# Decoder layer on one core: down-weight sums of the first feed-forward part from DRAM to DRAM, X sums kept on chip, output splits in the first down product

## The chip, the cores and the metric

The kernel runs on one core of a Trainium2 chip, in one launch. The metric is the device time of that launch in microseconds (us); lower is better. The time before is the median of three runs. TensorE (PE) multiplies matrices, VectorE (DVE), ScalarE (ACT) and GpSimd (POOL) do the elementwise work, and DMA transfers are issued through queues: SyncE's (SP) for weights and intermediates, GpSimd's for the sums of down weights.

## The reference

One layer in float32, for a sequence of 512 tokens with model width 1024 and feed-forward width 2816 (22 tiles of 128, taken as 11 pairs):

```
def swiglu(x, w_gate, w_up, w_down):
    return (jax.nn.silu(x @ w_gate) * (x @ w_up)) @ w_down

h = rms_norm(x, ffn1_pre)
x = x + 0.5 * rms_norm(swiglu(h, ffn1_w_gate, ffn1_w_up, ffn1_w_down), ffn1_post)
h = rms_norm(x, mix_pre)
x = x + rms_norm(token_mixer(h, ...), mix_post)     # sparse and dilated attention, gated
h = rms_norm(x, ffn2_pre)
x = x + 0.5 * rms_norm(swiglu(h, ffn2_w_gate, ffn2_w_up, ffn2_w_down), ffn2_post)
```

## The kernel before

**Matrix products.** Each float32 operand is split into a high part, cast by ScalarE (line 125), and the rest, subtracted by VectorE (line 126). `mm3` adds three matmuls for a product: high by high, high by low, low by high (lines 148, 149, 150). Both feed-forward parts run through one function, `ffn`, and multiply 2x2 blocks by a scheme of seven products in place of eight, with sums of blocks as operands. A pair of tiles of the gate and up weights takes the products P1, P2, P6, P5, P7, P4, P3, of 24 matmuls with 256 columns each: 168 matmuls a pair. `prep` makes a product's weight operand ready two products ahead: a block of 128x1024, or a sum of blocks (line 488 makes the first of these, for P6), then the split into `whi` and `wlo`.

**Weights.** All weight blocks come through SP's queue, in the order of use, into a ring `raw` of six half tiles. `refill` (line 311) issues the next block when the one before it in that half tile has been used, so a block's issue stands on SP's queue between the stores that other code puts there.

**Outputs of a pair.** `finished` copies the product banks (line 523, ScalarE), adds them and applies silu. After P3, `sums` makes from the two outputs `ev` and `od` three operands for the down products: X (in the one buffer `CB`, or in `PT`), the sum kept in `ev` and Y (lines 388 to 391, VectorE). `od`, X and Y are stored to DRAM (lines 392, 394, 397, SP's queue); where X of a pair is kept on chip it is listed in `kept`, which holds pairs 4 to 10 in the second part and none in the first. `ev` is cast and split at once into two slots named by `E_TAGS`. The first two pairs run without the seven products of the scheme ("plain"), pairs 2 to 10 in the loop.

**Sums of down weights.** The down projection is again seven products, B11, T2, T3, T1, B21, B22, T4, over the 11 pairs each. Four of them take sums of quarters of the down weight, which the kernel makes itself in `td`: td[2] and td[3] of two quarters each, td[0] = td[2] plus another one, td[1] = td[0] plus another one. For the second part, the mixer makes them in `table_sums`: copies and accumulating transfers on GpSimd's queue, from DRAM to DRAM, three pairs in one transfer, five steps for a group. In the first part `weight_sums` makes them as the loop goes: GpSimd's queue loads quarters of one pair into `PT` slots (line 361), accumulates other quarters onto them (line 351, an accumulating transfer too), and at the next step SP's queue stores the results to `td` (line 356). What each step does is listed in `SUMS`. `sums_behind` puts a one-column copy on GpSimd that reads an operand of the pair just finished, and lets the step's transfers be issued only after that copy and after the last store of `od`.

**Down products.** `product` in `ffn_down` goes through the pairs two at a time: split of the weight block, refill, matmuls, and after each pair a call of `side`, which splits the stored operands of later products (`split_next`, staged back from DRAM by `stage`). In B11 it splits an X at every second pair. In the last product T4 the `side` function is `settle`: after pairs 1 and 2 it updates a token tile of the residual x (line 761, whose factor GpSimd computes as a power, line 169), after pair 3 it finishes both tiles (norm, transposes or output). In T4 the weights of the last six pairs are only split as they come, and held: their matmuls follow for one token tile after the other (`tail` is 6).

A scheduler sets the order of each engine's instructions from the program's order and its own costs; the code gives the priority and the dependences. A slot is free again when the last reader of its content is done.

Of the kernel before, what the change touches and what calls it, by code (L numbers as in the profile page):

```python
# [12 lines left out]
F32 = mybir.dt.float32  # L13
# [14 lines left out]
NF = DFF // P  # L28
# [7 lines left out]
SUMS = [((0, 1), (), ())] + [((n + 1,), (n,) if n > 1 else (0, 1), (n - 1,) if n > 2 else (0, 1) * (n == 2)) for n in range(1, 13)]  # L36
# [11 lines left out]
E_TAGS = ["Q"] * 4 + ["KA"] * 4 + ["KB"] * 4 + ["x"] * 8 + ["of"] * 2  # L48
T_TAGS = ["SP"] * 11 + ["dm"]
# [9 lines left out]
class Layer:  # L59
# [257 lines left out]
    def ffn(self, gu, wd, td, post, finish, xsrc, aside=None, opened=None):  # L317
# [5 lines left out]
        later = {}  # L323
# [24 lines left out]
        def weight_sums(n):  # L348

            put = nc.gpsimd.dma_start  # L350
            add = lambda dst, src: put(dst, src, accum_op=OP.add)
            part = lambda q, e, h: wd[e, h, :, q]
            store, self.unstored = self.unstored, []
            keep = lambda i, q, t: self.unstored.append((td[i, :, q], t))
            for dst, t in store:
                nc.sync.dma_start(dst, t)
            new, one, two = [[q for q in v if q < NP] for v in SUMS[n]]
            for q in new:
                later[q] = r = [self.slot("PT") for _ in range(2)]
                for e in range(2):  # L360
                    put(r[e], part(q, e, 1))
            for h, qs in ((1, one), (0, two)):
                for q in qs:
                    add(later[q][0], part(q, 1, h))
                    keep(1 - h, q, later[q][0])
            for q in new:
                r = later[q]
                add(r[1], part(q, 0, 1))
                add(r[0], part(q, 0, 0))
                for e in range(2):  # L370
                    keep(2 + e, q, r[e])

# [11 lines left out]
        def sums(p, ev, od):  # L384

            h = slice(0, 256), slice(256, 512)
            x, y = self.slot("CB" if opened or p < KEEP else "PT"), self.slot("ring")
            nc.vector.tensor_sub(x[:, h[0]], ev[:, h[1]], od[:, h[1]])
            nc.vector.tensor_sub(x[:, h[1]], ev[:, h[0]], ev[:, h[1]])
            nc.vector.tensor_sub(ev[:, h[1]], x[:, h[0]], ev[:, h[0]])  # L390
            nc.vector.tensor_add(y[:, 0:256], od[:, h[0]], ev[:, h[1]])
            self.last_store = nc.sync.dma_start(self.odram[p], od).ins
            if opened or p < KEEP:
                nc.sync.dma_start(self.sxdram[p], x)
            else:
                kept[p] = x
            nc.sync.dma_start(self.ydram[p // 2][:, h[p % 2]], y[:, 0:256])
            hi, lo = [self.slot(e_tags.pop(0), F32R) for _ in range(2)]
            self.split(hi, lo, ev)
            E.append((hi, lo))  # L400

        def extra(p):
            if opened:
                sums_behind(E[p][0][:, 0:1].bitcast(F32), p + 1)

        def sums_behind(src, n):
            mark = self.sbt("mark", [P, 1])
            behind = nc.gpsimd.tensor_copy(mark, src).ins
            with self.tc.issue_after(behind), self.tc.issue_after(self.last_store or behind):
                weight_sums(n)  # L410

        banks = dict(opened["banks"]) if opened else {}
        if opened:
            tops = opened["tops"]
            self.unstored, self.last_store = [], None
# [58 lines left out]
        def last_sums():  # L474
            if opened:
                weight_sums(len(SUMS) - 1)

# [40 lines left out]
        def finished(p, name):  # L518
# [35 lines left out]
        self.ffn_down(E, kept, wd, td, post, finish, xsrc, aside, opened, last_sums)  # L554
# [78 lines left out]
    def ffn_down(self, E, kept, wd, td, post, finish, xsrc, aside, opened, last_sums):  # L633
# [36 lines left out]
        def product(a, wname, banks, start, stop, side=None, tail=0, keep=None, between=None):  # L670
# [8 lines left out]
            for k0 in range(0, NP, 2):  # L679
# [3 lines left out]
                if keep and k0 + m > NP - tail:  # L683
                    for j in range(m):
                        w = [self.slot(keep.pop(0), F32R) for _ in range(2)]
                        self.split(w[0], w[1], src[:, j])
                        held.append((k0 + j, w))
                    self.refill(r)
                    continue
                hi, lo = self.wsplit(src, [m, S])  # L690
                self.refill(r)
                for j in range(m):
# [20 lines left out]

        a = [self.bank("F") for _ in range(2)]
        product(half(E, 0), "B11", a, True, False, lambda k: k % 2 == 0 and split_next("X"))
# [7 lines left out]
        last_sums()  # L723
# [473 lines left out]
    def table_sums(self, wd, td, call):  # L1197

        put = self.nc.gpsimd.dma_start
        for b in range(0, NF // 2, 3):  # L1200
            q = slice(b, min(b + 3, NF // 2))
            step = call - b
            if step in (0, 1):
                for i, e, h in ((2, 0, 1), (3, 1, 1), (0, 1, 1), (1, 1, 0))[2 * step:2 * step + 2]:
                    put(td[i, :, q], wd[e, h, :, q])
            elif step == 2:
                put(td[2, :, q], wd[0, 0, :, q], accum_op=OP.add)
                put(td[3, :, q], wd[0, 1, :, q], accum_op=OP.add)
            elif step == 3:
                put(td[0, :, q], td[2, :, q], accum_op=OP.add)  # L1210
            elif step == 4:
                put(td[1, :, q], td[0, :, q], accum_op=OP.add)
# [415 lines left out]
    def run(self, out):  # L1628
# [10 lines left out]
        def boundary(post, pre, store, tags=None, shift=0):  # L1639
# [3 lines left out]
            def finish(t, gain):  # L1643
# [3 lines left out]
                if pre is not None:  # L1647
# [8 lines left out]
                   lambda m: self.table_sums(a["d2"], td[1], m))  # L1656
# [43 lines left out]
```

## Time and profile before

| what | value |
|---|---|
| runs shown | 1145.02, 1139.07, 1142.3 us; median 1142.3 |
| the profiled execution: its time, its span | 1139.46 us, 1137.7 us |
| granted TensorE clock, mean | 0.997 |
| busy in the span: PE, DVE, ACT, POOL | 97%, 78%, 56%, 15% |
| moved by DMA | 227.54 MB: 185.72 MB on SP's queue, 40.38 MB on GpSimd's |

The span runs from the first to the last instruction. The opening takes until about 37 us, the plain pairs until 51.65, the loop of the first part until about 239, its seven down products until about 362; the mixer follows, and the second part's loop lies within 844 to 1000 us, its down products behind it until the end. A row of a timeline gives the start, the duration, engine and line, the operation and its operands, and in brackets how long the engine had been idle ahead of it and whose end released it. L numbers are the line numbers of the kernel. "PEclk" is the clock that TensorE was granted, as a share of the full one; "x12" counts instructions that began in a stretch.

### The profile page before, as it was taken

What the parts mean: (1) busy time and instruction counts of PE and PEld (TensorE: products, weight loads), DVE (VectorE), ACT (ScalarE), POOL (GpSimd) and SP (SyncE); (2) the same over time, 40 slices, a digit from 0 to 9 for tenths busy, and PEclk for the clock granted to TensorE, in tenths of its full rate; (3) what the DMA queues carried; (4) which work ended last, traced back from release to release, by engine and by line L of the source; (5) the groups of instructions that cost most, each with busy time, mean ns of one, the idle gap of its engine ahead of it and who ended that gap; (6) DMA issues with size and microseconds to landing.
All of it is one profiled execution on the core that took longest, in us unless ns stands there. A gap on an engine that the chain in (4) does not pass through costs nothing.

```text
span 1137.7 us, 18596 instructions
## 1 busy us (share of the span) xinstructions
PE 1103.4 (97%) x6863; PEld 978.9 (86%) x6863; DVE 882.2 (78%) x1554; ACT 639.4 (56%) x1151; POOL 168.2 (15%) x220
## 2 busy tenths in 40 slices
PE   8989999999999999999999999999999999999996
PEld 7889999987878987777888898887989999998884
DVE  5979999987777889687554566876888989879564
ACT  7445555565564778676555634644435555557452
POOL 0423222230011054564000000000000000000000
PEclk9999999999999999999999999999999999999999
DMA  9999999999864669995134425383234434379761
GB/s 348 269 251 273 267 280 264 285 338 315 296 189 133 189 208 283 294 260 118 53 115 131 122 85 157 121 292 135 78 116 135 144 117 148 112 221 327 255 201 75
DMA packets 118411, 227.54 MB, mean 200 GB/s; under 512 B 21904, under 2 KB 51632, under 8 KB 118320
## 3 DMA queue, kind: packets, MB, share of 16 engines
q1 hardware_dynamic: 105472, 185.72, 49.1%
q0 software_dynamic: 12704, 40.38, 15.4%
q8 instruction: 54, 0.88, 0.3%
q14 instruction: 37, 0.30, 0.1%
q10 hardware_dynamic: 144, 0.26, 0.1%
HBM read 191.66 MB, written 57.72 MB: 219 GB/s over the span
## 4 chain that ended last, share of the span: by engine, by line
PE 64%; DVE 16%; DMA 9%; issue 5%; ACT 4%; POOL 2%; SPq 0%; DVEq 0%; POOLq 0%; ACTq 0%
PE pb_F L150 8%; PE pb_F L149 8%; PE pb_F L148 8%; DVE wlo L126 5%; PE pb_S L150 5%; PE pb_S L149 5%; PE pb_S L148 5%; PE pb_T L149 4%; PE pb_T L150 4%; PE pb_T L148 4%; DMA raw<-in_gu_dram 3%; PE pb_V L148 2%; PE pb_V L149 2%; DMA tdram<-in_d_dram 2%; PE pb_V L150 2%
## 5 line engine op out<-in xcount | busy, mean ns | idle before, releaser
L126 DVE TENSOR_TENSOR wlo<-raw,whi 128x1024 fp32r<-128x1024 f32 (+2 forms) x237 | 281.1, 1189 | 117.9 <-ACT whi L125 112.1
L125 ACT CAST whi<-raw 128x1024 fp32r<-128x1024 f32 (+2 forms) x237 | 241.5, 1021 | 204.9 <-PE pb_F L149 54.6
L148 PE MATMUL pb_F<-xhl_t,whi 128*128 128x512 f32 (+1 forms) x440 | 155.3, 353 | 1.7 <-DVE Q_s L1340 1.0
L150 PE MATMUL pb_F<-xhl_t,wlo 128*128 128x512 f32 (+1 forms) x440 | 154.3, 351 | 0.8 <-DVE wlo L126 0.7
L149 PE MATMUL pb_F<-xhl_t,whi 128*128 128x512 f32 (+1 forms) x440 | 154.0, 350 | 0.0
L169 POOL TENSOR_TENSOR rs_t<-rs_t,mhalf_t 128x1 f32<-128x1 f32 x20 | 12.8, 641 | 601.0 <-DVE rs_t L165 600.9
L148 PEld LDWEIGHTS pb_F<-xhl_t,whi 128*128 128x128 f32 x440 | 83.0, 189 | 11.8 <-DVE Q_s L1340 1.2
L150 PEld LDWEIGHTS pb_F<-xhl_t,wlo 128*128 128x128 f32 x440 | 82.8, 188 | 11.6 <-DVE wlo L126 2.0
L149 PEld LDWEIGHTS pb_F<-xhl_t,whi 128*128 128x128 f32 x440 | 82.8, 188 | 9.7 <-issue 0.2
L150 PE MATMUL pb_S<-xhl_t,wlo 128*128 128x256 f32 (+1 forms) x280 | 84.4, 302 | 3.0 <-DVE wlo L126 2.9
L148 PE MATMUL pb_S<-xhl_t,whi 128*128 128x256 f32 (+1 forms) x280 | 84.4, 301 | 0.0
L149 PE MATMUL pb_S<-xhl_t,whi 128*128 128x256 f32 (+1 forms) x280 | 84.2, 301 | 0.0
L1087 POOL TENSOR_SCALAR SP_s<-SP_s,st_t 128x384 f32<-128x384 f32 (+2 forms) x48 | 51.4, 1145 | 71.7 <-DVE st_t L1023 62.4
L150 PEld LDWEIGHTS pb_S<-xhl_t,wlo 128*128 128x128 f32 x280 | 53.2, 190 | 5.8 <-DVE wlo L126 3.6
L150 PE MATMUL pb_T<-xhl_t,wlo 128*128 128x256 f32 x200 | 56.0, 280 | 0.4 <-DVE wlo L126 0.4
L148 PE MATMUL pb_T<-xhl_t,whi 128*128 128x256 f32 x200 | 55.8, 279 | 0.0
L149 PE MATMUL pb_T<-xhl_t,whi 128*128 128x256 f32 x200 | 55.8, 279 | 0.0
L148 PEld LDWEIGHTS pb_S<-xhl_t,whi 128*128 128x128 f32 x280 | 53.4, 191 | 2.5 <-ACT V_s L523 0.2
L149 PEld LDWEIGHTS pb_S<-xhl_t,whi 128*128 128x128 f32 x280 | 53.2, 190 | 2.2
L148 PE MATMUL pb_S<-SP_s,whi 128*128 128x256 f32 x160 | 44.6, 279 | 2.6 <-ACT V_s L523 2.6
L125 ACT CAST whi<-tmp_t 128x1024 fp32r<-128x1024 f32 x36 | 37.8, 1050 | 16.5 <-ACT W_s L381 5.0
L126 DVE TENSOR_TENSOR wlo<-tmp_t,whi 128x1024 fp32r<-128x1024 f32 x36 | 43.9, 1219 | 1.4 <-ACT whi L125 1.3
(812 smaller groups left out, 3252.2 us busy)
## 6 DMA issues: line engine op xcount, KB each, us to landing
raw<-in_gu_dram SPq DMA_DIRECT2D x84, 512.0 KB, 4.5
raw<-tdram SPq DMA_DIRECT2D x40, 512.0 KB, 5.0
raw<-in_w_in_dram SPq DMA_DIRECT2D x18, 1024.0 KB, 5.3
PT_s<-in_d_dram POOLq DMA_DIRECT2D x66, 256.0 KB, 6.8
raw<-in_d_dram SPq DMA_DIRECT2D x30, 512.0 KB, 4.6
tdram<-in_d_dram POOLq DMA_DIRECT2D x18, 768.0 KB, 10.8
tdram<-PT_s SPq DMA_DIRECT2D x44, 256.0 KB, 4.5
odram<-W_s SPq DMA_DIRECT2D x22, 256.0 KB, 3.1
```

Of the source, the lines that this page charges most:

```text
L125: self.last_cast = self.nc.scalar.copy(dsthi, src).ins
L126: self.nc.vector.tensor_sub(dstlo, src, dsthi.bitcast(F32))
L148: mm(out, lhi, rhi, start=start, stop=False, skip_group_check=skip)
L149: mm(out, lhi, rlo, start=False, stop=False, skip_group_check=skip)
L150: mm(out, llo, rhi, start=False, stop=stop, skip_group_check=skip)
L169: nc.gpsimd.tensor_tensor(out=r, in0=v, in1=self.mhalf, op=OP.pow)
L1087: self.last_pool = nc.gpsimd.tensor_scalar(pp, pp, st[:, 1, t:t + 1], None, op0=OP.mult).ins
```

## The change

- `weight_sums` and `last_sums` are gone. The first part calls `table_sums` too, which now takes one group of three pairs and one step; `SUMS` lists which (group, step) go out after the opening and after each pair: 12 entries, so that the last goes out after pair 10. All of these are transfers from DRAM to DRAM on GpSimd's queue; they wait for the one-column copy alone. Nothing of them is on SP's queue.
- In the first part, too, X of pairs 4 to 10 stays in `PT` slots, which `weight_sums` needed before. It is not stored nor staged back.
- In the first part the outputs `ev` of pairs 3 to 10 (`LATER`) are put into `KB` and `x` slots, and cast and split not by `sums` but by `halves_of` within B11, ahead of the pairs that need them; B11 splits an X at every fourth pair.
- In T4 (both parts) `settle` does both updates after pair 3, with the scaling of d[1] that stood ahead of T4, and finishes after pair 5. For this `side` is also called for pairs that are held.

```
-SUMS = [((0, 1), (), ())] + [((n + 1,), (n,) if n > 1 else (0, 1), ...) for n in range(1, 13)]
+SUMS = [((0, 0),), ((0, 1), (1, 0)), ((0, 2), (1, 1)), ((0, 3), (1, 2)), ((0, 4), (2, 0)), ((1, 3), (2, 1)), ((1, 4), (2, 2)),
+        ((2, 3), (3, 0)), ((2, 4), (3, 1)), ((3, 2),), ((3, 3),), ((3, 4),)]
+LATER = 3
+LATER_TAGS = ["KB"] * 4 + ["x"] * 4, ["KA"] * 2 + ["of"] * 2 + ["x"] * 4 + ["KB"] * 4 + ["x"] * 3 + ["SP"]
...
-            x, y = self.slot("CB" if opened or p < KEEP else "PT"), self.slot("ring")
+            x, y = self.slot("CB" if p < KEEP else "PT"), self.slot("ring")
...
-            if opened or p < KEEP:
+            if p < KEEP:
                 nc.sync.dma_start(self.sxdram[p], x)
             else:
                 kept[p] = x
...
+            if p >= later:
+                E.append(ev)
+            else:
...
-            with self.tc.issue_after(behind), self.tc.issue_after(self.last_store or behind):
-                weight_sums(n)
+            with self.tc.issue_after(behind):
+                for g, step in SUMS[n]:
+                    self.table_sums(wd, td, 3 * g, step)
...
-                st["ev"], st["od"] = self.slot("ring"), self.slot("W")
+                st["ev"] = self.slot(LATER_TAGS[0][p - later] if p >= later else "ring")
+                st["od"] = self.slot("W")
...
+        def halves_of(k0):
+            for k in range(max(later, k0 + 2), min(k0 + 4, NP)):
+                hi, lo = [self.slot(e_tags.pop(0), F32R) for _ in range(2)]
+                self.split(hi, lo, E[k])
+                E[k] = hi, lo
...
-        product(half(E, 0), "B11", a, True, False, lambda k: k % 2 == 0 and split_next("X"))
+        product(half(E, 0), "B11", a, True, False, lambda k: k % 4 == 0 and split_next("X"), ahead=halves_of)
...
-        scaled(1, 1, d[1])
         def settle(k):
-            if k in (1, 2):
-                update(k - 1, (a[k - 1], d[k - 1]))
-            elif k == 3:
+            if k == 3:
+                scaled(1, 1, d[1])
+                for t in range(2):
+                    update(t, (a[t], d[t]))
+            elif k == 5:
                 for t in range(2):
                     finish(t, gain[1])
```

What this does to the order on SP's queue, at the end of pairs 0 and 1 (stores of Y, of weight sums, of `od` and X, and the refills of `raw`), before:

```order
L397 DMA ydram<-ring_s 128x256
L356 DMA tdram_94<-PT_s 128x512 x2
L311 DMA raw<-in_gu_dram 128x1024
L392 DMA odram<-W_s 128x512
L394 DMA sxdram<-CB_s 128x512
L356 DMA tdram_94<-PT_s 128x512
L397 DMA ydram<-ring_s 128x256
L356 DMA tdram_94<-PT_s 128x512 x3
L311 DMA raw<-in_gu_dram 128x1024 x4
```

And after:

```order
L375 DMA ydram<-ring_s 128x256
L314 DMA raw<-in_gu_dram 128x1024
L370 DMA odram<-W_s 128x512
L372 DMA sxdram<-CB_s 128x512
L375 DMA ydram<-ring_s 128x256
L314 DMA raw<-in_gu_dram 128x1024 x4
```

The six stores of weight sums, which stood ahead of refills, are gone; the rest keeps its order.

On VectorE at the end of pair 9 (adds of product banks, X and the other sums, splits of weights and of outputs), before:

```order
L382 TENSOR_TENSOR ring_s<-ring_s,V_s 128x256
L388 TENSOR_TENSOR CB_s<-ring_s,W_s 128x256
L389 TENSOR_TENSOR CB_s<-ring_s 128x256
L390 TENSOR_TENSOR ring_s<-CB_s,ring_s 128x256
L126 TENSOR_TENSOR wlo<-raw,whi 128x1024
L391 TENSOR_TENSOR ring_s<-W_s,ring_s 128x256
L126 TENSOR_TENSOR x_s<-ring_s,x_s 128x512
L382 TENSOR_TENSOR ring_s<-ring_s,V_s 128x256
L126 TENSOR_TENSOR wlo<-raw,whi 128x1024 x2
```

And after:

```order
L360 TENSOR_TENSOR x_s<-x_s,V_s 128x256 x2
L366 TENSOR_TENSOR PT_s<-x_s,W_s 128x256
L367 TENSOR_TENSOR PT_s<-x_s 128x256
L129 TENSOR_TENSOR x_s<-KB_s,x_s 128x512
L368 TENSOR_TENSOR x_s<-PT_s,x_s 128x256
L129 TENSOR_TENSOR wlo<-raw,whi 128x1024
L369 TENSOR_TENSOR ring_s<-W_s,x_s 128x256
L129 TENSOR_TENSOR x_s<-KB_s,x_s 128x512
L129 TENSOR_TENSOR KB_s<-x_s,KB_s 128x512
L129 TENSOR_TENSOR wlo<-raw,whi 128x1024
L129 TENSOR_TENSOR x_s<-x_s 128x512
L129 TENSOR_TENSOR wlo<-raw,whi 128x1024
```

Four splits of outputs (into `x` and `KB` slots) stand between the weight splits, where one stood.

On VectorE in T4 of the second part (the norm's factor, splits of held weights, scaling of d[1], updates of x), before:

```order
L165 TENSOR_SCALAR rs_t<-ss_t 128x1
L126 TENSOR_TENSOR SP_s<-raw,SP_s 128x512
L761 SCALAR_TENSOR_TENSOR x_s<-pb_F,rs_t,x_s 128x512
L754 TENSOR_TENSOR pb_V<-pb_V,CP_s 128x512
L761 SCALAR_TENSOR_TENSOR x_s<-pb_S,rs_t,x_s 128x512
L126 TENSOR_TENSOR wlo<-raw,whi 128x1024
```

And after:

```order
L168 TENSOR_SCALAR rs_t<-ss_t 128x1
L129 TENSOR_TENSOR SP_s<-raw,SP_s 128x512
L129 TENSOR_TENSOR wlo<-raw,whi 128x1024
L743 TENSOR_TENSOR pb_V<-pb_V,CP_s 128x512
L750 SCALAR_TENSOR_TENSOR x_s<-pb_F,rs_t,x_s 128x512
L750 SCALAR_TENSOR_TENSOR x_s<-pb_S,rs_t,x_s 128x512
```

The last weight split of the product now stands ahead of the updates.

More of the change, by code (lines that the diff above doesn't have):

```diff
@@ L35 @@
 KEEP = 4
-SUMS = [((0, 1), (), ())] + [((n + 1,), (n,) if n > 1 else (0, 1), (n - 1,) if n > 2 else (0, 1) * (n == 2)) for n in range(1, 13)]
+SUMS = [((0, 0),), ((0, 1), (1, 0)), ((0, 2), (1, 1)), ((0, 3), (1, 2)), ((0, 4), (2, 0)), ((1, 3), (2, 1)), ((1, 4), (2, 2)),
+        ((2, 3), (3, 0)), ((2, 4), (3, 1)), ((3, 2),), ((3, 3),), ((3, 4),)]
 GATES_AHEAD = 4
@@ L322, in ffn @@
         NP = NF // 2
-        later = {}
+        later = LATER if opened else NP
         def blk(p, h, f):
@@ L346, in mms @@
                 self.mm3(b[:, c], w[0][n][:, j], w[1][n][:, j], self.xh[k][:, c], self.xl[k][:, c], k == 0, k == KT - 1)
[L348 to L371, printed above, removed]
         e_tags, t_tags = list(E_TAGS), list(T_TAGS)
@@ L397, in sums @@
             nc.sync.dma_start(self.ydram[p // 2][:, h[p % 2]], y[:, 0:256])
-            hi, lo = [self.slot(e_tags.pop(0), F32R) for _ in range(2)]
-            self.split(hi, lo, ev)
-            E.append((hi, lo))
+            if p >= later:
+                E.append(ev)
+            else:
+                hi, lo = [self.slot(e_tags.pop(0), F32R) for _ in range(2)]
+                self.split(hi, lo, ev)
+                E.append((hi, lo))
         def extra(p):
             if opened:
-                sums_behind(E[p][0][:, 0:1].bitcast(F32), p + 1)
+                sums_behind((E[p] if p >= later else E[p][0].bitcast(F32))[:, 0:1], p + 1)
         def sums_behind(src, n):
@@ L553, in ffn @@
             finished(p, name)
-        self.ffn_down(E, kept, wd, td, post, finish, xsrc, aside, opened, last_sums)
+        self.ffn_down(E, later, kept, wd, td, post, finish, xsrc, aside, opened)
     def xop(self, k, c):
@@ L631, in scaled_sums, with ffn_down @@
         yield
-    def ffn_down(self, E, kept, wd, td, post, finish, xsrc, aside, opened, last_sums):
+    def ffn_down(self, E, later, kept, wd, td, post, finish, xsrc, aside, opened):
         nc = self.nc
@@ L668, in split_next, with product @@
             parts[nm].append((hi, lo))
-        def product(a, wname, banks, start, stop, side=None, tail=0, keep=None, between=None):
+        def product(a, wname, banks, start, stop, side=None, tail=0, keep=None, between=None, ahead=None):
             held = []
@@ L688, in product @@
                     self.refill(r)
+                    if side:
+                        side(k0 + m - 1)
                     continue
@@ L691, in product @@
                 self.refill(r)
+                if ahead:
+                    ahead(k0)
                 for j in range(m):
@@ L1195, in nsa, with table_sums @@
             fillers()
-    def table_sums(self, wd, td, call):
+    def table_sums(self, wd, td, b, step):
         put = self.nc.gpsimd.dma_start
[L1200 to L1212, printed above, removed]
+        q = slice(b, min(b + 3, NF // 2))
+        if step in (0, 1):
+            for i, e, h in ((2, 0, 1), (3, 1, 1), (0, 1, 1), (1, 1, 0))[2 * step:2 * step + 2]:
+                put(td[i, :, q], wd[e, h, :, q])
+        elif step == 2:
+            put(td[2, :, q], wd[0, 0, :, q], accum_op=OP.add)
+            put(td[3, :, q], wd[0, 1, :, q], accum_op=OP.add)
+        elif step == 3:
+            put(td[0, :, q], td[2, :, q], accum_op=OP.add)
+        elif step == 4:
+            put(td[1, :, q], td[0, :, q], accum_op=OP.add)
     def merge_unit(self, u):
@@ L1655, in run @@
         self.mixer(*boundary(a["mix_post"][0], a["ffn2_pre"][0], self.x2dram, AFTER_MIX, SHIFT),
-                   lambda m: self.table_sums(a["d2"], td[1], m))
+                   lambda m: [self.table_sums(a["d2"], td[1], b, m - b) for b in range(0, NP, 3)])
         self.ffn(a["gu2"], a["d2"], td[1],
```

9 lines of the change are left out of this document (3 added, 6 removed).

## The prediction

> **What bounds the kernel now.** I read the page first, then the busy time by stretches, TensorE's waits in the first part, the timelines of each engine around the two longest of them, and the transfers by stretch.
>
> ```profile
> span 1137.7 us, 18596 instructions
> PE 1103.4 (97%) x6863; PEld 978.9 (86%) x6863; DVE 882.2 (78%) x1554; ACT 639.4 (56%) x1151; POOL 168.2 (15%) x220
> PE 64%; DVE 16%; DMA 9%; issue 5%; ACT 4%; POOL 2%; SPq 0%; DVEq 0%; POOLq 0%; ACTq 0%
> ```
>
> TensorE is busy in 97% of the span; all its idle time together is 34 us. A change that leaves its 6863 matmuls alone, as this one does, can win only from those 34 us and from time at a reduced clock. By stretches (header, then the first part's pairs 2 to 4, pairs 4 to 10, and the second part's pairs):
>
> ```profile
> core 0: us, PE busy (x) PEld busy (x) DVE busy (x) ACT busy (x) POOL busy (x), PEclk, DMA share, GB/s
> 51.65:128.70 77.05, 71.64 (x601) 70.90 (x599) 68.12 (x96) 36.54 (x52) 22.72 (x27) 0.98 0.94 270
> 130.30:232.10 101.80, 101.79 (x864) 101.79 (x864) 99.01 (x138) 54.72 (x76) 29.73 (x36) 1.00 0.94 276
> 844.00:998.60 154.60, 153.96 (x1346) 153.04 (x1345) 140.21 (x179) 82.95 (x117) 0.00 (x0) 1.00 0.42 132
> ```
>
> From 130 us on TensorE never stops in the first part: 101.80/864 = 0.1178 us a matmul, 19.8 us a pair of 168. The second part's same loop takes 154.60/1346 = 0.1149, so there are two paces at the same granted clock, which no row explains. The first stretch is the odd one: 601 matmuls at 0.1178 are 70.8 us, and it took 77.05. That excess of 6.2 us is what the change can reach. Its places are:
>
> ```profile
> 60.43 0.39 PE L148 MATMUL pb_S<-SP_s,whi 128*128 128x256 f32 x1 [2.62 <-ACT V_s L523]
> 74.88 0.39 PE L150 MATMUL pb_S<-xhl_t,wlo 128*128 128x256 f32 x1 [2.63 <-DVE wlo L126]
> 76.00:78.00 2.00, 2.00 (x12) 2.00 (x11) 2.00 (x3) 0.00 (x0) 0.00 (x0) 0.50 1.10 272
> 78.00:80.00 2.00, 2.00 (x13) 2.00 (x13) 2.00 (x3) 0.81 (x2) 0.00 (x0) 0.64 1.00 331
> ```
>
> Two waits, A (2.62) and B (2.63), and behind them a stretch at a granted clock of 0.50 and 0.64, which costs 2 x 0.50 + 2 x 0.36 = 1.7 us. Together 7.0; the remaining 0.8 comes back where matmuls there ran at the faster pace.
>
> **Down-weight sums from DRAM to DRAM: wait B.** SP's queue, VectorE and GpSimd before B:
>
> ```profile
> 57.15 0.86 POOL L351 DMA_DIRECT2D PT_s<-in_d_dram  x1 [0.21 <-issue]
> 57.80 0.38 SPq L394 DMA_DIRECT2D sxdram<-CB_s  x1
> 60.05 0.32 SPq L356 DMA_DIRECT2D tdram<-PT_s  x1
> 60.46 1.32 SPq L397 DMA_DIRECT2D ydram<-ring_s  x1
> 65.31 1.30 SPq L356 DMA_DIRECT2D tdram<-PT_s  x3
> 66.73 0.44 SPq L311 DMA_DIRECT2D raw<-in_gu_dram  x1
> 72.46 1.23 DVE L488 TENSOR_TENSOR tmp_t<-raw 128x1024 f32<-128x1024 f32 x1 [6.16 <-DMA raw<-in_gu_dram]
> SPq L356 <- DMA PT_s<-in_d_dram: 17.2, 11, 3.5
> ```
>
> The store L356 waits until an accumulation that GpSimd issued at 57.15 has landed (65.3). The weight block that VectorE needs at 66.3 stands behind it in the queue, goes out at 66.73 and lands at 72.4. In the new order no such store is in SP's queue: the block is next after the y store, so out by about 60.5, or 57.9 when A is gone too. VectorE's L488 must begin 2.63 sooner for TensorE not to wait, and with A gone, when TensorE needs it sooner by that too, by 72.46 - 2.63 - 2.6 = 67.2: some 9.3 us after an issue at 57.9. What it takes depends on what else is under way:
>
> ```profile
> q0 software_dynamic: 2511, 5.51, 57.4%
> q0 software_dynamic: 5441, 11.54, 36.7%
> q0 software_dynamic: 4476, 22.31, 80.0%
> q1 hardware_dynamic: 10420, 26.42, 85.7%
> raw<-in_gu_dram SPq DMA_DIRECT2D x25, 512.0 KB, 6.6
> raw<-in_gu_dram SPq DMA_DIRECT2D x27, 512.0 KB, 3.9
> gdram<-ring_s SPq DMA_DIRECT2D x4, 256.0 KB, 7.5
> gdram<-ring_s SPq DMA_DIRECT2D x16, 256.0 KB, 2.7
> ```
>
> (Transfers by stretch: GpSimd's queue in 36:80, 80:240 and 420:530, where the mixer does these very sums from DRAM to DRAM; SP's queue in 240:330; then a weight block in 80:240 and in 860:1010; a store in 420:530 and over the whole span.) GpSimd's sums through SBUF cost 25.3 us (57.4% of 44) and 58.7 us (36.7% of 160) of all 16 engines, the 44 stores of 0.26 MB at 77.1/26.42 = 2.9 us a MB another 34: about 118 us. The same sums from DRAM to DRAM move 44 x 2 x 0.26 = 23 MB at 88/22.31 = 3.94 us a MB: 91 us. The seven X sums kept on chip remove 14 transfers, 3.7 MB, 11 us. So the load falls by some 38 us of about 210. But it bunches: after pair 0 four copies of 768 KB go out at once (12.4 us of all engines) and after pair 1 four more transfers, where before two loads and four accumulations of 256 KB went out. A weight block behind these takes between 3.9 us (undisturbed) and 10.8 (3.9 x 7.5/2.7, the stretch being the store's in the mixer); near the 6.6 that it takes beside sums now, I say 6.5. It then lands at about 64.4 (from 57.9) or 67.0 (from 60.5), inside the limit. B goes with its slow clock: -2.6 - 1.7 = -4.3; the range is 0 to -4.3.
>
> **Wait A** comes from a store too:
>
> ```profile
> 43.76 0.33 SPq L394 DMA_DIRECT2D sxdram<-CB_s  x1
> 51.08 0.43 DVE L389 TENSOR_TENSOR CB_s<-ring_s 128x256 f32<-128x256 f32 x1 [2.61 <-DMA sxdram<-CB_s]
> 59.28 0.62 ACT L125 CAST Q_s<-ring_s 128x512 fp32r<-128x512 f32 x1 [2.11 <-DVE ring_s L390]
> 59.80 0.58 ACT L523 COPY V_s<-pb_S 128x512 f32<-128x512 f32 x1
> ```
>
> VectorE waits 2.61 us for pair 0's X store to release the one CB buffer; it is late by as much at L390, ScalarE's cast waits for that, and the bank's copy stands behind the cast. Pair 0 still stores X after the change. What is under way from 43 to 47 us, though, is 2 copies of 768 KB issued at 36.8 (1.57 MB x 3.94 = 6.2 us, over by about 45) instead of eight transfers of 256 KB that reach to 52.8. The store then needs between 2.7 and 7.5 us (the rows above); nearer the first, since the next copies go out only at 46.8. At 4.7 us or less the wait is gone. I take -2.2; range 0 to -2.6.
>
> **The pace.** With both waits gone the weights stand ready early, as from 130 us on, where the pace is 0.1178. The 0.8 us of faster matmuls goes: +0.8. A, B and pace: -2.2 - 4.3 + 0.8 = -5.7.
>
> **Loads later in the loop.** From pair 2 on three transfers of 768 KB follow each pair's sums, issued about when VectorE's next block is. That block is already waited for where nothing disturbs it: the second part's load of 3.9 us makes VectorE idle 1.5 us a pair.
>
> ```profile
> 876.01 1.23 DVE L488 TENSOR_TENSOR tmp_t<-raw 128x1024 f32<-128x1024 f32 x1 [1.49 <-DMA raw<-in_gu_dram]
> 130.31 0.38 PE L148 MATMUL pb_T<-SP_s,whi 128*128 128x256 f32 x1 [1.34 <-ACT V_s L523]
> ```
>
> Between 0 (as now, 0.01 us idle in 101.8) and, at 10.8 us, 6.9 over the undisturbed 3.9, on every second pair: 4 x (6.9 - 1.0) = +24. The 1.0 is the slack of two pairs, 19.8 us each here against 19.3 (168 x 0.1149) there. Most of the pairs issue the block ahead of the sums, so I take the near end: +0.8. The wait of 1.34 at 130 us stays; its copy stands behind the same cast.
>
> **Casts and splits of the outputs, X splits every fourth step.** The split (ScalarE 0.62, VectorE 0.69) moves but is not removed. In the new order those of pairs 3 and 4 stand where they stood, and four are bunched at the end of pair 9, where one was: three more at a pitch of 0.6 make 1.8 us on VectorE.
>
> ```profile
> 230.56 1.23 DVE L126 TENSOR_TENSOR wlo<-raw,whi 128x1024 fp32r<-128x1024 f32 x1 [0.30 <-ACT whi L125]
> 233.38 1.23 DVE L126 TENSOR_TENSOR wlo<-raw,whi 128x1024 fp32r<-128x1024 f32 x1 [1.58 <-ACT whi L125]
> 250.87 0.86 POOL L351 DMA_DIRECT2D PT_s<-in_d_dram  x1
> ```
>
> VectorE idles 0.30 + 1.58 = 1.9 us at that place: 0, and +1.8 if that cover is gone. VectorE's load falls by 0.6 us in pairs 5 to 8, but TensorE does not wait for it there: 0. GpSimd's last sum, td[1] += td[0] behind pair 10, replaces the accumulation at 250.87 ahead of the iotas for which VectorE waits; it waits for the sum one step earlier, issued a pair sooner: 0, with +-1 as the bound.
>
> **The order at the end** (settle, both parts):
>
> ```profile
> 1117.45 0.50 PE L149 MATMUL pb_T<-wlo,KA_s 128*128 128x512 f32 x1 [1.28 <-DVE wlo L126]
> 1114.26 0.75 DVE L761 SCALAR_TENSOR_TENSOR x_s<-pb_F,rs_t,x_s 128x512 f32<-128x512 f32 x1 [0.44 <-POOL rs_t L169]
> 1116.18 1.22 DVE L126 TENSOR_TENSOR wlo<-raw,whi 128x1024 fp32r<-128x1024 f32 x1
> PE pb_F L219 <- DVE tmp_t L214: 0.5, 1, 0.5
> ```
>
> In the second part TensorE's wait of 1.28 is for a split that stands behind an update, which waits for GpSimd's power. The new order has the split first: at 1113.8 it is done 2.4 us sooner, TensorE continues to the end of the program: -1.3, range 0 to -1.3 (nothing between there and the end would take it back, save the last chain's squares, which follow the last matmul anyway). In the first part the same move leaves one wait of 0.5 at the transposes to win (chain unclear behind it): -0.2.
>
> **Sum.** -5.7 + 0.8 - 1.3 - 0.2 = -6.4 us against the profiled execution: span 1137.7, 1139.46 with what lies around it, so about 1133. The median of the runs shown is 1142.3, 2.8 above that execution; on it the same difference gives 1136.
>
> **A rule that speaks against it.** The Trainium skill (DMA: Bandwidth & Descriptors, Queues, rings and completion order) says that a DMA engine takes turns between queues packet by packet, so a weight block waits for whole packets of the sums. The trace agrees in kind: the store at 7.5 us beside the sums against 2.7 is such a stretch. By that rule alone, at 10.8 us a load, the sum is the third rival's. The same skill (SBUF — State Buffer, SBUF: two separate sides) says that VectorE and GpSimd lock a shared port for a whole instruction; the one-column copy of 5.08 us before the row at 250.87 agrees, and by it the iotas would come up to 1 us later here, inside the bound given.
>
> **Rivals.** First, B stays: the burst after pair 0 holds the block until 71 us though SP sends it sooner. For: those 12.4 us of queued copies at 47. Against: blocks and sums share engines now as well, at 6.6. Then -6.4 + 4.3 = -2.1: about 1140. Second, the loop of the first part runs at the second part's pace: 1512 matmuls x (0.1178 - 0.1149) = -4.4 more: about 1131.5; for it speaks that the pace there belongs to VectorE's idling for blocks, which this change brings; against, that the weights are ready sooner. Third, on the other side: VectorE waits for the block at L488 after each second pair. It decides from where those four loads take more than 3.9 + 1.0 + 7.2/4 = 6.7 us (7.2 is the sum without the +0.8 of the loads); at 10.8 it is -7.2 + 24 = +17: about 1159. For: the mixer's store; against: the sums begin only when the block is under way, the load as a whole falls by 38 us, and loads of 6.6 us beside the sums cost TensorE nothing now.
>
> **How the numbers follow.** As sum 0.5, B stays 0.2, faster pace 0.12, blocks late 0.14, else 0.04. The likeliest case's own range is 1132 to 1140. A measurement tells about 0.5% (5.7 us: runs lie between 1139.1 and 1145.0) from no change, so 1136.6 and 1148 are the bounds. Faster: two thirds of the first case, all of the faster pace: 0.47, with the tail. Same: the rest of these, B stays and the rest of the tail: 0.40. Slower: nearly all of late blocks, 0.13. Range 1130 to 1146: it leaves out the far half of late blocks and the tail below.
>
> **What would show it.** Right: no idle of TensorE at 55 to 75 us of more than 0.5, clock 1.00 there, VectorE's L488 of pair 3 at once behind its predecessor; no L356 kind of store; the last weight wait near the end gone. Wrong: L488 rows with idle of 2 us and more behind raw<-in_gu_dram, weight blocks above 7 us to landing between 80 and 240, the first product waiting for wlo behind the iotas, or the loop's matmuls off 0.1178.

## The result, and the profile after

| | time, us | ratio to before, 95% interval |
|---|---|---|
| before, 4 runs | 1142.8 (1139.1 to 1145.0) | |
| changed, 4 runs | 1149.1 (1148.6 to 1150.6) | 1.0061 [1.0032, 1.0089] |

The changed kernel is 0.6% slower: outside the range given, on the other side of no change. The page, first lines and shares of the chain:

```profile
span 1146.8 us, 18400 instructions
PE 1106.8 (97%) x6863; PEld 979.7 (85%) x6863; DVE 879.5 (77%) x1554; ACT 638.7 (56%) x1151; POOL 130.7 (11%) x186
PE 59%; DVE 21%; DMA 10%; issue 4%; ACT 4%; POOL 2%; DVEq 0%; POOLq 0%; SPq 0%; ACTq 0%
```

Both traces hold the same 6863 matmuls, so the start of the k-th can be set against the start of the k-th (read from the traces; "step" is what the stretch lost):

```
matmul    before     after   difference   step
   250     57.20     57.84     +0.64
   300     65.96     64.95     -1.01      -1.65   wait A
   425     85.08     86.06     +0.98      +1.99   wait B and the clock behind it
   675    113.85    114.40     +0.55      -0.43
   750    122.46    133.30    +10.85     +10.30   wait C and the clock behind it
   950    147.37    156.17     +8.80      -2.05   the wait of 1.34 at 130 is gone; a faster pace
  2250    357.84    369.87    +12.03      +3.23   steps of 1.3 us at most, in the loop and the down products
  5900    960.61    972.74    +12.13      +0.10   mixer and the second part's loop
  6862   1129.35   1138.56     +9.21      -2.92   end of the second part
```

One place makes the loss: matmuls 675 to 750, in pair 4. (What makes the +3.23 stays open: TensorE's waits from 150 us to the end of the down products add up to 5.7 us before and 6.7 after.) The timeline there, with the two earlier waits (TensorE, VectorE, SP's queue):

```profile
59.43 0.39 PE L151 MATMUL pb_S<-SP_s,whi 128*128 128x256 f32 x1 [0.97 <-ACT V_s L500]
...
74.98 0.58 PE L153 MATMUL pb_S<-xhl_t,wlo 128*128 128x256 f32 x1 [3.74 <-DVE wlo L129]
...
124.06 0.58 PE L153 MATMUL pb_S<-xhl_t,wlo 128*128 128x256 f32 x1 [8.02 <-DVE wlo L129]
...
72.56 1.22 DVE L465 TENSOR_TENSOR tmp_t<-raw 128x1024 f32<-128x1024 f32 x1 [7.27 <-DMA raw<-in_gu_dram]
...
121.64 1.22 DVE L465 TENSOR_TENSOR tmp_t<-raw 128x1024 f32<-128x1024 f32 x1 [9.15 <-DMA raw<-in_gu_dram]
...
62.56 1.22 DVE L129 TENSOR_TENSOR wlo<-raw,whi 128x1024 fp32r<-128x1024 f32 x1
...
63.80 0.33 SPq L314 DMA_DIRECT2D raw<-in_gu_dram  x1
...
108.64 0.33 SPq L314 DMA_DIRECT2D raw<-in_gu_dram  x1
```

(L465 is L488 of before, L314 is L311, L129 is L126.) The block that VectorE needs at 112.5 went out at 108.64 and came at 121.6, after 12.9 us. TensorE stood 8.02 us. Behind both waits it was granted half the clock (busy times by stretch):

```profile
74.00:76.00 2.00, 1.02 (x5) 1.03 (x6) 2.00 (x3) 0.00 (x0) 0.00 (x0) 0.50 0.44 140
...
78.00:80.00 2.00, 2.00 (x11) 2.00 (x11) 2.00 (x3) 0.50 (x2) 0.00 (x0) 0.50 0.69 236
80.00:82.00 2.00, 2.00 (x17) 2.00 (x16) 2.00 (x4) 0.96 (x1) 0.00 (x0) 0.81 0.78 258
...
124.00:126.00 2.00, 1.95 (x9) 1.95 (x10) 2.00 (x2) 0.00 (x0) 0.00 (x0) 0.50 1.01 379
126.00:128.00 2.00, 2.00 (x11) 2.00 (x11) 2.00 (x4) 0.00 (x0) 0.00 (x0) 0.50 0.83 277
128.00:130.00 2.00, 2.00 (x17) 2.00 (x16) 2.00 (x5) 1.47 (x2) 0.00 (x0) 0.87 0.91 270
```

Behind C that is 1.95 x 0.50 + 2 x 0.50 + 2 x 0.13 = 2.2 us on top of the 8.0. What was under way is on GpSimd's queue:

```profile
88.71 1.06 POOL L389 COPY mark_t<-KA_s 128x1 f32<-128x1 f32 x1 [26.31 <-ACT KA_s L128]
89.71 0.83 POOL L1198 DMA_DIRECT2D tdram<-tdram  x1
90.26 1.14 POOL L1195 DMA_DIRECT2D tdram<-in_d_dram  x1
90.79 1.44 POOL L1196 DMA_DIRECT2D tdram<-in_d_dram  x1
91.32 1.10 POOL L389 COPY mark_t<-KB_s 128x1 f32<-128x1 f32 x1
98.04 0.81 POOL L1200 DMA_DIRECT2D tdram<-tdram  x1 [5.62 <-DMA tdram<-tdram]
98.56 1.34 POOL L1193 DMA_DIRECT2D tdram<-in_d_dram  x2
109.42 0.25 POOL L389 COPY mark_t<-KB_s 128x1 f32<-128x1 f32 x1 [9.51 <-DVE KB_s L360]
```

The copy behind pair 3 ran at 91.32, right after pair 2's, and not some 20 us later. `extra` lets it read column 0 of pair 3's output. With the deferred splits that output is the plain tile, whose first half the silu and product behind P2 write (L360, the row at 109.42 names it for pair 4): at the beginning of the pair's outputs, not at the end of `sums`. So steps 3 and 4 met, six transfers of 768 KB within 10 us, and step 5 came at 109.9. (The sums of a step wait not for the copy alone: the row at 98.04 waited for the sum that it reads.) Weight blocks met these as well: two that went out at 98.55 and 99.97 landed 12.0 and 14.4 us later, at 110.5 and 114.3, so the block of 108.64 also stood behind them on SP's own queue.

### The profile page after: what moved, and what is told of

It reads as the page before. It is cut to its first block, busy times and chain, and to the rows that moved or that the text cites. A ratio compares the mean times of both kernels' runs of the same rounds, so it can differ in the third digit from the quotient of the medians.

```text
span 1146.8 us, 18400 instructions
## 1 busy us (share of the span) xinstructions
PE 1106.8 (97%) x6863; PEld 979.7 (85%) x6863; DVE 879.5 (77%) x1554; ACT 638.7 (56%) x1151; POOL 130.7 (11%) x186
## 4 chain that ended last, share of the span: by engine, by line
PE 59%; DVE 21%; DMA 10%; issue 4%; ACT 4%; POOL 2%; DVEq 0%; POOLq 0%; SPq 0%; ACTq 0%
PE pb_F L153 8%; PE pb_F L151 8%; PE pb_F L152 8%; DVE wlo L129 7%; PE pb_S L153 5%; PE pb_S L151 5%; PE pb_S L152 5%; DMA raw<-in_gu_dram 4%; PE pb_T L152 4%; PE pb_T L153 4%; PE pb_T L151 4%; PE pb_V L151 2%; PE pb_V L152 2%; PE pb_V L153 2%; DMA tmp_t<-in_x_dram 1%
## 5 line engine op out<-in xcount | busy, mean ns | idle before, releaser
L129 DVE TENSOR_TENSOR wlo<-raw,whi 128x1024 fp32r<-128x1024 f32 (+2 forms) x237 | 280.4, 1185 | 120.0 <-ACT whi L128 115.9
L151 PEld LDWEIGHTS pb_S<-xhl_t,whi 128*128 128x128 f32 x280 | 54.6, 195 | 2.7 <-DVE V_s L509 0.3
L152 PEld LDWEIGHTS pb_S<-xhl_t,whi 128*128 128x128 f32 x280 | 54.6, 195 | 2.2
L465 DVE TENSOR_TENSOR tmp_t<-raw 128x1024 f32<-128x1024 f32 x18 | 22.0, 1224 | 37.8 <-DMA raw<-in_gu_dram 37.8
```

What stands on the lines that cost most here:

```text
L129: self.nc.vector.tensor_sub(dstlo, src, dsthi.bitcast(F32))
L151: mm(out, lhi, rhi, start=start, stop=False, skip_group_check=skip)
L152: mm(out, lhi, rlo, start=False, stop=False, skip_group_check=skip)
L465: nc.vector.tensor_add(s1, blk(p, 0, 1), blk(p, 1, 1))
```

## Experiments

Each kernel ran beside the kernel before on the same chip; ratios are to that. In the kernels that change the release alone, nothing but the operand of GpSimd's one-column copy differs from the kernel that they start from, on any engine.

**Release at the pair's end.**

```
-                sums_behind((E[p] if p >= later else E[p][0].bitcast(F32))[:, 0:1], p + 1)
+                sums_behind(E[p][:, 256:257] if p >= later else E[p][0].bitcast(F32)[:, 0:1], p + 1)
```

> The changed kernel, but GpSimd's one-column copy behind pairs 3 to 10 reads column 256 of the pair's even output, which sums writes at the pair's end, in place of column 0, which the silu after P2 writes at its beginning. Order on every engine as in the changed kernel. Theory M (the sums go out a pair too early, so that nine transfers of 768 KB meet within 20 us and hold pair 4's block for 12.9 us): that block takes under 9 us, the wait of 8.0 us at 116 and the slow clock behind it go, TensorE's matmul 750 begins some 10 us sooner, wait B (3.7 us at 71) stays; time about 1139 to 1141, 8 to 10 below the changed kernel. Rival S (transfers of 768 KB hold the blocks whenever they go out): blocks of 10 us and more every second pair, waits of 2 to 5 us remain, 1144 to 1149. Rival D (the splits moved to B11 cost it): no change, 1149.

Measured: 1153.5 us, 1.011 [1.0081, 1.0138], slower still. Wait C went as theory M said (matmul 750 began at 122.58, 10.7 us sooner), but three new waits came, at 135, 180 and 225, which M had not foreseen and S had in kind (it gave blocks of 10 us and 1144 to 1149; they took 8.1 to 9.0). M explains wait C, but not the loss.

**No deferral.**

```
-        later = LATER if opened else NP
+        later = NP
```

> The changed kernel without the deferred casts and splits: each pair's output is split in sums as before, and the copy that releases the weight sums reads the split output, thus at the pair's end. Sums from DRAM to DRAM, seven X on chip and the order at the end stay. Theory M: as with the late copy, 1139 to 1141, for the release is at the pair's end here too; the two differ by under 2 us, so that the moved splits as such are worth nothing. Rival S: 1144 to 1149, waits of TensorE behind blocks remain. Rival D: the moved splits cost time by themselves: this one is faster than the late copy by over 3 us.

Measured: 1137.3 us, 0.9964 [0.9944, 0.9983]: faster than before, and 16 us faster than the late copy, on which M had wanted no more than 2. By its words rival D had won here. The two timelines at the same boundary, behind pair 4, spoke for something else. The late copy (GpSimd, SP's queue, VectorE, TensorE):

```profile
127.02 0.25 POOL L389 COPY mark_t<-KB_s 128x1 f32<-128x1 f32 x1 [14.50 <-DVE KB_s L368]
127.51 0.83 POOL L1198 DMA_DIRECT2D tdram<-tdram  x1 [0.24 <-issue]
128.05 1.33 POOL L1193 DMA_DIRECT2D tdram<-in_d_dram  x2
...
128.72 0.33 SPq L314 DMA_DIRECT2D raw<-in_gu_dram  x1
...
137.48 1.23 DVE L465 TENSOR_TENSOR tmp_t<-raw 128x1024 f32<-128x1024 f32 x1 [6.71 <-DMA raw<-in_gu_dram]
...
139.90 0.58 PE L153 MATMUL pb_T<-xhl_t,wlo 128*128 128x256 f32 x1 [4.60 <-DVE wlo L129]
```

No deferral:

```profile
129.69 1.06 POOL L389 COPY mark_t<-KB_s 128x1 f32<-128x1 f32 x1 [16.46 <-ACT KB_s L128]
130.69 0.83 POOL L1198 DMA_DIRECT2D tdram<-tdram  x1
131.24 1.32 POOL L1193 DMA_DIRECT2D tdram<-in_d_dram  x2
...
130.74 0.33 SPq L314 DMA_DIRECT2D raw<-in_gu_dram  x1
...
134.24 1.23 DVE L465 TENSOR_TENSOR tmp_t<-raw 128x1024 f32<-128x1024 f32 x1 [0.32 <-DMA raw<-in_gu_dram]
```

The same three transfers and the same block. Where the sums go out 1.2, 0.7 and 0.2 us ahead of the block, it takes 8.7 us; where they go out with it, 0.5 and 1.0 us behind, 3.4. Without deferral the copy reads the split's high half and waits for ScalarE's cast: it starts 1.05 us ahead of the block in place of 1.70, and takes 1.06 us in place of 0.25, so the first transfer goes out with the block. From this came theory P: what counts is which goes out first.

**Smaller burst at the start** (on top of the late copy):

```
-SUMS = [((0, 0),), ((0, 1), (1, 0)), ((0, 2), (1, 1)), ((0, 3), (1, 2)), ((0, 4), (2, 0)), ((1, 3), (2, 1)), ((1, 4), (2, 2)),
-        ((2, 3), (3, 0)), ((2, 4), (3, 1)), ((3, 2),), ((3, 3),), ((3, 4),)]
+SUMS = [((0, 0),), ((0, 1),), ((0, 2),), ((0, 3), (1, 0)), ((0, 4), (1, 1)), ((1, 2), (2, 0)), ((1, 3), (2, 1)),
+        ((1, 4), (2, 2), (3, 0)), ((2, 3), (3, 1)), ((2, 4), (3, 2)), ((3, 3),), ((3, 4),)]
```

> The late copy, and the sums of the second group of three pairs begin two steps later: 2, 2, 2, 3, 3, 4, 3, 5, 3, 3, 1, 1 transfers in the twelve steps in place of 2, 4, 4, 3, 3, 3, 3, 3, 3, 2, 1, 1. Theory M with bursts: between 46 and 62 us four large transfers are under way and not eight, pair 2's block (issued at about 63.8, when VectorE's split frees its half tile) takes 5 to 6 us in place of 8.7, VectorE's L465 begins at about 69.5, TensorE's wait B falls from 3.7 to 1 or less and its slow clock goes: 3 to 5 us less than the late copy, 1135 to 1137. Rival (the block is late by the half tile's release alone): B keeps 2.5 us or more, time as with the late copy.

Measured: 1153.4 us, 1.0117 [1.0085, 1.015]. A miss: with half the transfers ahead of it, 4.2 and 3.7 us earlier, the block of wait B (pair 2's in the expectation; VectorE needs it for pair 3) still took 7.5 us, against 8.7 with the late copy, and the later waits stayed, behind blocks of 9.3 to 10.1. Half as much in front shortened that block by 1.2 us only.

**No sums at all.**

```
-                for g, step in SUMS[n]:
-                    self.table_sums(wd, td, 3 * g, step)
+                pass
...
-        self.ring_of(gu, wd, td, (), 4)
+        self.ring_of(gu, wd, [wd[0, 0], wd[0, 1], wd[1, 0], wd[1, 1]], (), 4)
```

> The changed kernel without the weight sums of the first part: nothing on GpSimd's queue there, and the four down products that need sums read single quarters of the weight (these sums are left out of what is computed). All else in place, the early copy too. Every theory in which transfers are the cause: no wait over 1 us of TensorE between 45 and 240 us save the one that the code's own order makes, blocks take 3.5 us, pair 2's block lands at about 67.3 and wait B is under 0.5; 12 to 16 us less than the changed kernel, 1133 to 1137. Rival D (moved splits): still above 1142.

Measured: 1128.1 us, 0.9886 [0.9861, 0.9912]: 13 us below before, some 20 below the changed kernel, with the deferred splits in it; 5 us below the range expected. So the sums' transfers carry the whole loss, and D is out as its cause. An order of these transfers that costs nothing could be expected to come to about this time.

**Release behind the block's half tile.** The copy that releases steps 2 to 10 reads a column of the split (P7 of the next pair) that frees the block's half tile; the splits stay deferred.

```
+        self.last_lo = dstlo        # in split
...
         elif name in ("P7", "P4", "P3"):
-                self.refill(src)
+                self.refill(src); sums_behind(self.last_lo.bitcast(F32)[:, 0:1], p) if name == "P7" and opened else None
...
-            if opened:
+            if opened and p in (0, NP - 1):
```

> The changed kernel, deferred splits included; GpSimd's copy that releases step n (2 to 10) of the sums reads a column of the weight split that frees the half tile for VectorE's next L465 block, so that the block is issued ahead of the sums. Nothing else in the order of any engine differs. Theory P (what counts is which goes out first: a block that is issued before the sums takes 3.3 to 4.8 us, one that is issued 0.2 to 11 us behind them 8 to 13): no L465 block above 5 us, waits B (3.7 us at 71) and C (8.0 at 116) both under 1 us, no slow clock behind them; 14 to 18 us below the changed kernel, 1131 to 1135. Rival D (the deferred splits cost time by themselves): above 1143. Rival V (what counts is how much is under way in 20 us): blocks of 6 to 9 us remain, 1139 to 1146.

The same without deferral (with `later = NP` beside it):

> The same release behind the block's half tile, with the splits made in sums as before the change. Against the kernel without deferral (1137.3) only the early step after pair 1 moves, from 3 us ahead of pair 2's block to behind it. Theory P: that block takes 3.5 to 5 us in place of 9.8, wait B (4.8 us at 70) and its slow clock go: 5 to 7 us less, 1130 to 1132; within 2 us of the changed kernel with the same release. Rival V: B shrinks to 2 or 3 us, 1134 to 1136. Rival D: over 5 us faster than the changed kernel with the same release.

Measured: 1131.8 us, 0.9918 [0.989, 0.9947] with deferral, and 1129.9 us, 0.9892 [0.9863, 0.9921] without: 16 and 19 us below the changed kernel by the ratios, and both faster than before. The two intervals overlap, and the 2 us between them are under the 5 that D wanted, so D falls a second time. The profile of the one with deferral, at wait B's old place (GpSimd, SP's queue, VectorE), and then the stretch of pairs 2 to 4 (us, then the busy time of PE, PEld, DVE, ACT and POOL, the clock, the DMA share):

```profile
61.72 0.25 POOL L389 COPY mark_t<-wlo 128x1 f32<-128x1 f32 x1 [13.45 <-DVE wlo L129]
62.17 0.89 POOL L1195 DMA_DIRECT2D tdram<-in_d_dram  x1 [0.21 <-issue]
...
61.62 0.33 SPq L314 DMA_DIRECT2D raw<-in_gu_dram  x1
...
65.08 1.23 DVE L465 TENSOR_TENSOR tmp_t<-raw 128x1024 f32<-128x1024 f32 x1 [1.98 <-DMA raw<-in_gu_dram]
```

```profile
51.65:128.70 77.05, 76.32 (x646) 75.23 (x645) 70.27 (x99) 40.60 (x57) 13.39 (x17) 1.00 0.88 257
```

The block takes 3.4 us, A, B and C are gone, the clock stays at 1.00, and 646 matmuls begin where 601 did before.

**The early release, without deferral.**

```
-                sums_behind((E[p] if p >= later else E[p][0].bitcast(F32))[:, 0:1], p + 1)
+            self.evs = {p: ev}          # in sums
...
+                sums_behind(self.evs[p][:, 256:257] if p >= LATER else E[p][0].bitcast(F32)[:, 0:1], p + 1)
```

> The kernel without deferral, with the copy behind pairs 3 to 9 reading the second half of the even output before its cast, which lets the sums go out some 1.2 us earlier, ahead of the block. Theory P: as in the kernel with the late copy, blocks of every second pair take 8 to 9 us, three waits of TensorE of 4 to 5 us at about 135, 180 and 225 with a slow clock behind each: 1148 to 1155, thus 11 to 18 us for 1.2 us of earlier issue. Rival D (the deferral made the late copy slow): 1136 to 1139, no change. Rival V: 1136 to 1139 too, since as much is under way.

Measured: 1152.1 us, 1.0079 [1.0051, 1.0107]. As P said: blocks of 8.7, 8.4 and 8.4 us, and TensorE's waits at 137, 181 and 225. These were of 2.9, 2.5 and 2.3 us, though, not 4 to 5, and the clock fell behind the first alone; the profiled run, 1147.6 us, was the second fastest of seven. An order that differs by 1.2 us cost 13 to 15 us (by the ratios, by the medians), with the splits where they stood before the change.

**The order at the end alone** (on the kernel before).

```
-        scaled(1, 1, d[1])
...
-            if k in (1, 2):
-                update(k - 1, (a[k - 1], d[k - 1]))
-            elif k == 3:
+            if k == 3:
+                scaled(1, 1, d[1])
+                for t in range(2):
+                    update(t, (a[t], d[t]))
+            elif k == 5:
```

> The kernel before with the new order of updates in T4 alone (both parts). By the prediction: the wait of 1.28 us for the last weight split at the second part's end goes, as does up to 0.2 in the first: -1.3 to -1.5 us, 1139.3 on 1140.8. Rival: the last chain of squares, power and updates behind the last matmul takes it back, less than 0.5 us gained.

Measured: 1140.4 us, 0.9983 [0.9963, 1.0003]: about -1.9 us, with an interval that still holds no change. In the trace against before's, the steps from matmul 6775 to 6800 and from 6800 to 6825, in T4 of the second part, are 0.68 and 1.56 us shorter, 2.2 in all, and nothing gives that back. (Another 0.69 us between 6425 and 6450 lies ahead of T4, where the order on VectorE and ScalarE is the same in both.)

**The release behind the block, on the kernel before**, with its sums through SBUF:

```
-                self.refill(src)
+                self.refill(src); sums_behind(self.last_lo.bitcast(F32)[:, 0:1], p) if name == "P7" and opened else None
...
-            if opened:
+            if opened and p in (0, NP - 1):
                 sums_behind(E[p][0][:, 0:1].bitcast(F32), p + 1)
```

> The kernel before with the release of its weight sums (through SBUF, 256 KB each) moved behind the weight split that frees the half tile of the next L488 block. Theory P: nothing to gain from pair 3 on, where the sums already go out with the block or later and it takes 3.4 to 3.9 us; before pair 2's block the two loads of step 2 move behind it, but the store L356 that waits for an accumulation still stands ahead of it on SP's queue, so wait B stays at 1.5 us or more and wait A as it is: 0 to 2 us less, 1139 to 1142. Rival O (the order of release alone makes the gain, whatever way the sums take): 5 us or more less, below 1137.

Measured: 1139.3 us, 0.9989 [0.997, 1.0008]: no gain that can be told. From pair 4 on the sums went out with the block or behind it already. In its trace wait A is gone, for a cause that stays open, and wait B is 6.05 us in place of 2.63: a store L356 at 66.60 still stands ahead of the block, which went out at 68.02. So the order of release alone does not make the gain; all of it came only with both, sums off SP's queue and their release behind the block.

**X stored, with the release behind the block and no deferral:**

```
-            x, y = self.slot("CB" if p < KEEP else "PT"), self.slot("ring")
+            x, y = self.slot("CB" if opened or p < KEEP else "PT"), self.slot("ring")
...
-            if p < KEEP:
+            if opened or p < KEEP:
```

> The kernel without deferral with the release behind the block, but all X sums stored and staged back as before the change (3.7 MB more on SP's queue, one CB buffer). Theory P: the X stores go out behind the block or well ahead of it, blocks stay under 5 us: within 1.5 us of the same kernel with seven X on chip (1130). Rival X (the X sums on chip carry a good part of the gain): 2 us or more above it.

Measured: 1129.7 us, 0.9908 [0.9886, 0.9929]. The seven X on chip are worth nothing that can be told, as P expected.

**Early release, small transfers.** `table_sums` makes one transfer for each pair, three for a group:

```
-    def table_sums(self, wd, td, b, step):
+    def table_sums(self, wd, td, b, step, m=3):
+        for c in range(b, min(b + 3, NF // 2), m): self.table_part(wd, td, slice(c, min(c + m, NF // 2)), step)
```

> The kernel without deferral and with the copy 1.2 us early (1152 us), but each transfer of three pairs (768 KB) cut into transfers of one pair (256 KB), as many bytes in three times as many issues of some 0.53 us. Theory P with the amount issued ahead: in the 1.2 us before the block only two or three transfers of 256 KB go out and not three of 768 KB, the rest follows behind it; the block of every second pair takes 4.5 to 6 us in place of 8.7, TensorE's waits at 135, 180 and 225 shrink from 2.5 to 3.1 us to under 1.5: 1138 to 1146. Rival Q (any sums in front of the block hold it to their end, as the queue is served in order): still 8 us and 1150 or more.

Measured: 1139.0 us, 0.9985 [0.9972, 0.9999]: 11 to 13 us less than with 768 KB at a time, for the same bytes. Two blocks that went out 1.2 us behind the first transfers, with three and two of them ahead, took 5.1 and 5.7 us. Rival Q falls: the block of 5.1 us had three transfers ahead of it, and two of these landed 5.7 and 7.0 us after its issue, behind it. But the block of wait B, with eight transfers of 256 KB issued 0.5 to 4.2 us ahead, still took 8.0 us: it is not the size of one transfer alone that counts.

All blocks for L465 of pairs 3 to 10 (issue to landing in us, from each transfer in the traces):

| kernel | issued ahead of the sums, or with them | issued 1.2 us or more behind the first of the sums, of 768 KB |
|---|---|---|
| changed | 3.3 to 4.4 | 8.7 (B), 12.9 (C) |
| late copy | 3.3 to 3.5 | 8.7 (B), 8.7, 9.0, 8.1 |
| late copy, smaller burst | 3.3 to 3.5 | 7.5 (B), 9.3, 10.1, 9.3 |
| no deferral | 3.3 to 4.8 | 9.8 (B) |
| no deferral, early | 3.3 to 3.5 | 9.2 (B), 8.7, 8.4, 8.4 |
| behind the block, both | 3.4 to 4.0 | none |

## Why the prediction was wrong

- **Loads later in the loop** is the step that failed: +0.8 was taken, and the changed kernel lost 10.3 there. The reason given, that most pairs issue the block ahead of the sums, was read from the order before and from a trace in which the copy waited for a cast. The change put another tile under that copy: its code shows that the column is written behind P2. The third rival had the mechanism and gave 1159; its condition ("from 6.7 us on") held at one pair, with 12.9 us in place of the 10.8 that I took as the worst, and the slow clock behind the wait, 2.2 us, was not in its price. The argument against it, that the sums begin only when the block is under way, is the one that was wrong. In its place the runs showed that a block issued 1.2 us or more behind the first sums takes 7.5 us or more, and 12.9 with two steps of them at once.
- **Wait B** was to go (-4.3) and cost 2.0 us more. Two terms were off. I put the block's issue at 57.9 to 60.5, next in SP's queue; it went at 63.80, when VectorE's split of 62.56 had freed the half tile. In the trace of before that split ended at 64.8, so the store had held the block from there to 66.73 only. And it took 8.7 us, not 6.5, with four transfers of 768 KB issued 2.6 to 4.2 us ahead. B stays, the first rival, was right in kind. With the sums behind the block it did go: without deferral, that release shortens the stretch from matmul 350 to 375 by 6.7 us.
- **Wait A**: -1.65 between matmuls 250 and 300, against -2.2. The X store went out at 43.71 and landed at 49.98, 6.3 us later, above the 4.7 below which the wait would end; VectorE waited 1.66 in place of 2.61.
- **The pace**: +0.8 was not borne out. Matmuls 850 to 950 took 11.53 us after and 11.78 before, so the pace was faster there; small steps behind 950 took more than that back. The wait of 1.34 at 130, expected to stay, went in the changed kernel (and is back without deferral).
- **The order at the end**: -1.3 - 0.2 was taken, and T4 of the second part alone shows 0.68 + 1.56 = 2.2 in the trace of that edit. Right in kind, low in size; the runs' -1.9 is not told from no change.
- **Casts, splits, X on chip**: 0 holds to within some 2 us, by the pairs above: 1131.8 with deferral and 1129.9 without, 1129.7 with X stored. What the deferral did was to move the release.
- **The rule that was weighed.** The Trainium skill (DMA: Bandwidth & Descriptors, Queues, rings and completion order) has each DMA engine take turns between its queues packet by packet. The traces agree with it in part, as shown below: of some 5 us that a block lost, turns fit about 2. The 10.8 us a load that the prediction set beside the rule came nearer to C's 12.9 than the median of 6.6 us did, and no nearer to B's 8.7; it was read off a store in the mixer, not off turns, so this is in part luck. The median mixes two kinds: in the trace of before, blocks for the loop that went out ahead of the sums or with them took 3.4 to 3.9 us, those behind them 5.7 to 9.1.

The sum itself described a kernel one operand away: -6.4 was predicted, and with the release behind the block the ratio 0.9918 means -9.4 us, with an interval of -12.6 to -6.0. In that kernel's trace the stretches of A and B are 2.4 and 4.4 us shorter than before, where 2.2 and 4.3 were taken.

## What to carry to other kernels

When a transfer that an engine waits for shares the DMA engines with bulk transfers that have time, let the bulk go out behind it: bind its release to what frees the waited transfer's buffer, not to some operand that is ready at about that time. When a change swaps the tile behind a dependence, look up who writes the very column that is read. A median time to landing hides two kinds; split it by what had been issued ahead.

## What the runs showed of the hardware

A block of 512 KB that went out with three transfers of 768 KB, or up to 2.8 us ahead, took 3.3 to 3.6 us in the kernel without deferral (one 4.8), as long as without any sums (3.3 to 3.5). With the first of them 1.2 us ahead it took 8.1 to 9.0 (late copy, early release). With two or three transfers of 256 KB ahead it took 5.7 and 5.1, with eight 8.0.

The records of the single packets show why 1.2 us decide. A block without any sums moved its first packet 0.95 to 1.10 us after its issue and its last after some 3.1. The sums, issued 1.2 us ahead, moved their first packet 1.6 us after their own issue, thus 0.4 us after the block's, and the block's first came only 3.9 us after its issue (late copy, issue at 128.72): 99 packets of the sums, six on each engine, ran in between. Sums issued together with the block moved first 2.4 to 2.7 us after it, when most of the block was through. So what moves first counts, and the sums take longer from issue to first packet.

The DMA queues while such a block was under way, in the kernel with the late copy (128.7 to 137.4 us) and then in the one with small transfers (129.2 to 134.3; packets, MB, share of 16 engines):

```profile
q0 software_dynamic: 335, 1.87, 81.3%
q1 hardware_dynamic: 194, 0.56, 16.3%
```

```profile
q0 software_dynamic: 283, 0.53, 72.1%
q1 hardware_dynamic: 197, 0.56, 28.3%
```

A packet of GpSimd's queue (q0) took 0.813 x 16 x 8.7 / 335 = 0.34 us with the large transfers and 0.721 x 16 x 5.1 / 283 = 0.21 with the small. Of the packets on SP's queue (q1) 128 are the block's, of 4 KB each, eight on each engine, at 0.16 us; the others are small ones. If each of the eight waits for one packet of the sums, 8 x 0.34 = 2.7 us are added, and 8 x 0.21 = 1.7: estimates, against the measured 4.7 to 5.6 with the large transfers and 1.7 to 2.3 with the small (4.6 for the block behind eight). With the large ones they are too small. The block of 128.72 lost 2.9 us until its first packet, and 2.0 from there to its last (4.1 in place of 2.1). The second part fits turns packet by packet: the packets of the sums that ran meanwhile took 0.24 us, and 8 x 0.24 = 1.9, an estimate too. Why the block's queue got no turn in the first part stays open, and no run here changed the packets alone.

The slow clock, at 0.50 for 3.4 us or for two or three times that, followed every wait of TensorE from 3.4 to 8 us, and some of 2.6 to 3.1 but not all: behind the one of 2.9 us at 137 in the early kernel the clock fell to 0.50, behind those of 2.5 and 2.3 at 181 and 225 it stayed at 1.00, as it did behind one of 3.0 at 71 with the late copy. What decides it at that length stays open.
